# A decoder layer on one Trainium2 core: the pooling projection taken from x before its norm, with the token factors applied to the results

## The chip, the core and the metric

The kernel runs on one core of one Trainium2 chip. A core has five engines that work side by side, each through its own queue in order: TensorE (PE; matmuls, with its weight loads, PEld, overlapped), VectorE (DVE), ScalarE (ACT), GpSimd (POOL) and SyncE (SP), which here issues most transfers from HBM. Data lies in SBUF, 128 partitions wide; matmuls write PSUM, in banks of 128 x 512 floats. The metric is the time of one execution in microseconds (us) on the device, as the median of several.

## What is computed

One layer of a hybrid decoder, in fp32, on x of 512 tokens by 1024 channels. The input is normed, one wide projection gives everything that the three mixing branches and their gates need, and a gated FFN follows:

```python
def rmsnorm(x, g):
    xf = x.astype(jnp.float32)
    y = xf * lax.rsqrt(jnp.mean(xf * xf, axis=-1, keepdims=True) + NORM_EPS)
    return (y * g.astype(jnp.float32)).astype(x.dtype)

u = rmsnorm(x, ln1_g[i])
proj = u @ w_in[i]
q, k, v, pool_in, z, xbc, dt_raw, gate_pre = jnp.split(proj, split_idx, axis=-1)
y_a = dilated_attention_mixer(q, k, v, rel_bias) @ w_a[i]
y_b = pool_mixer(pool_in, pool_w[i], pool_scale[i]) @ w_b[i]
y_c = ssd_mixer(z, xbc, dt_raw, ...) @ w_c[i]
x = x + (gates[:, :, 0] * y_a + gates[:, :, 1] * y_b + gates[:, :, 2] * y_c) @ w_o[i]
x = x + conv_ffn(rmsnorm(x, ln2_g[i]), ...)
return rmsnorm(x, final_g)
```

`pool_mixer` takes means over the last 2, 4, 8 or 16 tokens of `pool_in` (1024 channels, four groups with a window each), subtracts `pool_in`, and multiplies by a small matrix per group. The change touches how u, and from it `pool_in`, come about. The factor of the norm belongs to a token, so it can be applied to a row of x before the projection, or to the token's results behind it.

## The kernel before

*Precision.* Every large product is made of three matmuls in a rounded format: each operand is split into a high part (rounded) and a low part (what the rounding left), and high x high, high x low and low x high are summed (`mm3`, L228). For a weight, ScalarE makes the high part (`cast`, L186, its line L195) and VectorE the low part (`lows`/`low`, L208 to L223, line L215). For the normed input, `uh` and `ul` (eight blocks of 128 channels, 512 tokens) are kept for the whole projection.

*Jobs.* The work is a list of jobs (`program`, L1422). A job has 1 MB of weights, say 256 columns: two chunks of 128 output channels by 512 tokens, 24 matmuls each. While a job runs, the low part of the next job's weights, the high part of the one after and the load of the third are put into the queues (`prepare`, L1624). There are two buffers of raw weights, three of high and two of low parts. The first four jobs are the pooling projection (eight chunks, `C_POOL`), then come the values of the first attention group (`v_jobs`, two jobs of 400 columns with tokens as output rows, each with half of the channel blocks), then queries and keys.

*Order.* The order on PE, ACT, DVE and POOL is that in which the program emits it (`manual_schedule`, L106); only SP is ordered by the framework. Work that trails behind a chunk is written as generators: `step()` (L156), called after each chunk, first runs what `second` holds (the second half of a cast), then starts one item of `waiting`, then moves each running generator to its next `yield`.

*Pooling chunk.* `pool_evac(m, ps)` (L771) copies the chunk out of its PSUM bank to `pu` on ScalarE (L775), GpSimd makes the window sums by doubling (L779 to L782: one to four additions `psw`), and two steps later VectorE subtracts (`pd`, L788), ScalarE rounds (`pdh`, L790) and VectorE makes the low part (`pdl`, L791). Four PSUM banks hold the chunks, so chunk m + 4 needs chunk m copied out.

*The start* (L1474 to L1613) is written out by hand. x arrives as four blocks of 128 tokens in two halves (`xin`). For blocks 0 and 1 ScalarE and VectorE sum the squares, a short chain (L1558 to L1564) gives a diagonal with the token factors, and TensorE turns and scales the block in one product with it (`turn_scale`, L1551). `turned` (L1519) multiplies by the gain, gives `uh` on ScalarE and `ul` on VectorE. Then `begin(n, lo, hi)` (L1526) runs chunks 0 to 3 of the pooling projection in halves of 256 tokens. Blocks 2 and 3 are scaled in place (L1587, L1589) and turned inside the second `begin`. GpSimd makes the low part of the first weights.

Of the kernel before, what the change touches and what calls it, by code (L numbers as in the profile page):

```python
# [16 lines left out]
P = 128  # L17
# [66 lines left out]
def trunk(ctx: ExitStack, tc, out, x, rel_bias, ln1_g, w_in, b_gate, w_a, pool_w, pool_scale, w_b,  # L84
# [682 lines left out]

    ramp = cpool.tile([P, 4, 16], F32, name="ramp")
    DP, YB = {}, {}

    def pool_evac(m, ps):  # L771
        g = m // 2
        w = 2 << g
        u = T("pu")
        act.copy(u, ps)  # L775
        cur, sh = u, 1
        while sh < w:
            nxt = T("psw")
            pool.tensor_tensor(nxt[:, sh:], cur[:, sh:], cur[:, :S - sh], OP.add)  # L779
            pool.tensor_copy(nxt[:, :sh], cur[:, :sh])  # L780
            cur, sh = nxt, sh * 2
        pool.tensor_tensor(cur[:, :w], cur[:, :w], ramp[:, g, :w], OP.mult)  # L782

        def later():
            yield
            yield
            d = T("pd")
            dve.scalar_tensor_tensor(d, cur, 1.0 / w, u, OP.mult, OP.subtract)  # L788
            dh, dl = T("pdh", F32R), T("pdl", F32R)
            act.copy(dh, d)  # L790
            dve.tensor_sub(dl, d, dh.bitcast(F32))  # L791
            DP[m] = (dh, dl)

        running.append(later())
# [678 lines left out]

    xin, warm = {}, small("warm", [P, 1])  # L1474

    def load_x(tb, eng=sp):
        for h in range(2):
# [12 lines left out]

    def warm_up(n):
        for i in range(n):
            pe.matmul(first[3][:, :P], ones, ones, start=True, stop=True)
# [11 lines left out]
    sp.dma_start(tri, c_tri)  # L1505
    rows_of_bias = bias_rows()

    def row_squares(tb, ss, n=1, eng=dve):

        for i in range(n):  # L1510
            squares(act, xin[tb + i, 0], ss[:, i:i + 1])
            squares(eng, xin[tb + i, 1], ss[:, n + i:n + i + 1])
        dve.tensor_tensor(ss[:, :n], ss[:, :n], ss[:, n:2 * n], OP.add)
        return ss[:, :n]

    def x_block(tb, k):
        return xin[tb, k // 4][:, (k % 4) * P:(k % 4 + 1) * P]

    def turned(k, lo, ps):  # L1519

        hh = uh[:, k, lo:lo + 256]
        act.mul(hh, ps, g1[:, k:k + 1])
        dve.scalar_tensor_tensor(ul[:, k, lo:lo + 256], ps, g1[:, k:k + 1], hh.bitcast(F32),
                                 OP.mult, OP.subtract)

    def begin(n, lo, hi, between=lambda early: None):  # L1526
        wh, wl = weights[n].split
        order = [(wh, uh, 0)]
        for k in range(1, KD):
            order += [(wh, uh, k), (wh, ul, k - 1)]  # L1530
        order.append((wh, ul, KD - 1))
        for part in (order, [(wl, uh, k) for k in range(KD)]):
            for a, b, k in part:
                for j in range(2):
                    pe.matmul(first[2 * n + j][:, lo:hi], a[:, k, j * P:(j + 1) * P], b[:, k, lo:hi],  # L1535
                              start=a is wh and b is uh and k == 0, stop=a is wl and k == KD - 1)
            between(part is order)
        if hi == S:
            for j in range(2):
                pool_evac(2 * n + j, first[2 * n + j])  # L1540
                step()


    warm_up(WARM)
    diag = [T("diag") for _ in range(2)]
    banks = [SM("uT") for _ in range(4)]

    def bank(k):
        return banks[k % 4][:, (k // 4) * 256:(k // 4) * 256 + 256]

    def turn_scale(tb, k):  # L1551
        pe.matmul(bank(k)[:, tb * P:(tb + 1) * P], x_block(tb, k), diag[tb][:, :P], start=True, stop=True)  # L1552

    for tb in range(2):
        s0, s1, v, sq, r, rt = (small(n, [P, 1]) for n in ("s0", "s1", "v", "sq", "r", "rt"))
        squares(act, xin[tb, 0], s0)
        squares((dve, act)[tb], xin[tb, 1], s1)
        dve.tensor_scalar(v, s0, 1.0 / D, EPS, OP.mult, OP.add)  # L1558
        dve.scalar_tensor_tensor(v, s1, 1.0 / D, v, OP.mult, OP.add)
        act.activation(sq, v, AF.Sqrt)  # L1560
        dve.reciprocal(r, sq)
        dve.scalar_tensor_tensor(rt, r, v, r, OP.mult, OP.mult)
        dve.tensor_scalar(rt, rt, -0.5, 1.5, OP.mult, OP.add)
        dve.tensor_scalar(diag[tb][:, :P], eye, r, rt, OP.mult, OP.mult)  # L1564
        if tb == 0:
            for k in range(KD):
                turn_scale(0, k)
    pe.transpose(first[2][:, :KD], g8[:KD, :P], eye[:KD, :KD])
# [8 lines left out]
    parts = lows(weights[1], 2)  # L1577


    ss = row_squares(2, small("ss", [P, 4]), 2)  # L1580
    next(parts)
    r = rstd_of(ss, 2, D)
    for tb in (2, 3):
        for h in range(2):
            t = xin[tb, h]
            if h:
                dve.tensor_scalar(t, t, r[:, tb - 2:tb - 1], None, OP.mult)  # L1587
            else:
                act.mul(t, t, r[:, tb - 2:tb - 1])  # L1589
    next(parts)  # L1590
    begin(0, 0, 256)

    def turns(early):
        if not early:
            return
        for k in range(4):
            banks[k] = SM("uT")
        for k in range(KD):
            for tb in range(2):
                pe.transpose(bank(k)[:, tb * P:(tb + 1) * P], x_block(2 + tb, k), eye)  # L1600
        for k in range(KD):
            turned(k, 256, bank(k))

    begin(1, 0, 256, turns)
    turn()
    fetch(weights[2])
    fetch(weights[3])
    begin(0, 256, S)
# [44 lines left out]
WARM = 12  # L1653

# [1 line left out]
_INS = ['x', 'rel_bias', 'ln1_g', 'w_in', 'b_gate', 'w_a', 'pool_w', 'pool_scale', 'w_b',  # L1656
# [26 lines left out]
```

## Time and profile before

| | us |
|---|---|
| median of 3 runs | 1042.7 (1042.38 to 1042.83) |
| the profiled execution, whole | 1044.23 |
| its span | 1042.4 |
| PE busy | 1030.2 |
| DVE busy | 645.8 |
| ACT busy | 466.9 |
| POOL busy | 151.1 |

The page gives the busy time of each engine, the chain of work that ended last, and groups of instructions by line. In a row of a group the columns are line, engine, operation, output and inputs by the program's names, shapes and count, then busy time in us and the mean of one in ns, then idle time of the engine just before and what ended it. In a row of the timeline the first number is the start in us, the second the length. A busy PE is not PE at its peak; GpSimd's spans are rough. The profile's times are those of one execution, whose whole time is a little over the span.

### The profile page before, as it was taken

What the parts mean: (1) busy time and instruction counts of PE and PEld (TensorE: products, weight loads), DVE (VectorE), ACT (ScalarE), POOL (GpSimd) and SP (SyncE); (2) the same over time, 40 slices, a digit from 0 to 9 for tenths busy, and PEclk for the clock granted to TensorE, in tenths of its full rate; (3) what the DMA queues carried; (4) which work ended last, traced back from release to release, by engine and by line L of the source; (5) the groups of instructions that cost most, each with busy time, mean ns of one, the idle gap of its engine ahead of it and who ended that gap; (6) DMA issues with size and microseconds to landing.
All of it is one profiled execution on the core that took longest, in us unless ns stands there. A gap on an engine that the chain in (4) does not pass through costs nothing.

```text
span 1042.4 us, 13096 instructions
## 1 busy us (share of the span) xinstructions
PE 1030.2 (99%) x5214; PEld 864.4 (83%) x5214; DVE 645.8 (62%) x864; ACT 466.9 (45%) x756; POOL 151.1 (14%) x125
## 2 busy tenths in 40 slices
PE   8999999999999999999999999999999999999997
PEld 8988878898888878888888888898888888878885
DVE  5563566684356658766768666767766566556645
ACT  5432554452464364557545233544444344433331
POOL 1680000000000004210152500002111111110110
PEclk9999999999999999999999999999999999999999
DMA  8345222126222344552243326642232322362332
GB/s 294 107 116 148 97 66 75 31 62 201 81 81 81 98 135 112 142 137 80 68 132 122 121 81 242 220 162 86 87 116 81 121 81 97 105 242 70 112 101 81
DMA packets 119788, 121.81 MB, mean 117 GB/s; under 512 B 5523, under 2 KB 101590, under 8 KB 119727
## 3 DMA queue, kind: packets, MB, share of 16 engines
q1 hardware_dynamic: 119135, 120.12, 36.4%
q8 instruction: 41, 0.67, 0.3%
q10 hardware_dynamic: 592, 0.86, 0.2%
q14 instruction: 20, 0.16, 0.1%
HBM read 115.07 MB, written 4.32 MB: 115 GB/s over the span
## 4 chain that ended last, share of the span: by engine, by line
PE 97%; DVE 1%; ACT 1%; DMA 0%; issue 0%; DVEq 0%; SPq 0%; ACTq 0%
PE pa L234 35%; PE pu L234 22%; PE pb L234 17%; PE pqk L234 9%; PE pa L1535 2%; PE p L234 2%; PE ps L662 1%; PE pu L1356 1%; PE ppw L234 1%; PE pt L690 1%; PE po L703 1%; PE py L988 1%; PE uT L1552 1%; PE pyo L995 1%; PE pst L974 0%; DMA xin<-in_x_dram 0%
## 5 line engine op out<-in xcount | busy, mean ns | idle before, releaser
L215 DVE TENSOR_TENSOR wl<-raw,wh 128x2048 fp32r<-128x2048 f32 (+3 forms) x95 | 217.1, 2287 | 73.9 <-ACT wh L195 41.7
L195 ACT CAST wh<-raw 128x1024 fp32r<-128x1024 f32 (+3 forms) x188 | 189.5, 1026 | 63.0 <-DVE raw L337 21.1
L234 PE MATMUL pa<-uh,wh 128*128 128x512 f32 x384 | 98.5, 398 | 0.0
L1192 DVE SCALAR_TENSOR_TENSOR hc<-pu,fcol,hc 128x510 f32<-128x510 f32 x88 | 65.8, 748 | 51.1 <-ACT hc L1189 49.5
L234 PE MATMUL pa<-ul,wh 128*128 128x512 f32 x384 | 94.9, 389 | 0.0
L234 PE MATMUL pa<-uh,wl 128*128 128x512 f32 x384 | 94.9, 389 | 0.0
L234 PEld LDWEIGHTS pa<-ul,wh 128*128 128x128 f32 x384 | 72.1, 188 | 15.2
L234 PEld LDWEIGHTS pa<-uh,wl 128*128 128x128 f32 x384 | 72.1, 188 | 15.0
L234 PE MATMUL pu<-uh,wh 128*128 128x512 f32 (+1 forms) x352 | 83.7, 380 | 0.0
L234 PE MATMUL pu<-ul,wh 128*128 128x512 f32 (+1 forms) x352 | 83.5, 379 | 0.0
L234 PE MATMUL pu<-uh,wl 128*128 128x512 f32 (+1 forms) x352 | 83.5, 379 | 0.0
L234 PEld LDWEIGHTS pa<-uh,wh 128*128 128x128 f32 x384 | 70.3, 188 | 14.7 <-issue 1.0
L234 PEld LDWEIGHTS pu<-uh,wh 128*128 128x128 f32 x352 | 64.1, 188 | 12.6 <-ACT uh L452 0.2
L234 PEld LDWEIGHTS pu<-ul,wh 128*128 128x128 f32 x352 | 64.2, 188 | 12.5
L234 PEld LDWEIGHTS pu<-uh,wl 128*128 128x128 f32 x352 | 64.2, 188 | 12.5
L1189 ACT ACTIVATE hc<-pu,fcol,fcol 128x512 f32<-128x512 f32 x40 | 31.2, 780 | 75.6 <-PE pu L234 75.4
L1197 POOL TENSOR_TENSOR hc<-hc 128x512 f32<-128x512 f32 x22 | 31.5, 1431 | 223.5 <-DVE hc L1192 169.3
L950 POOL TENSOR_TENSOR xd<-xc,dec 128x512 f32<-128x512 f32 x6 | 6.4, 1061 | 333.7 <-DVE xc L944 314.8
L1077 ACT ACTIVATE sg<-pa,col 128x512 f32<-128x512 f32 x24 | 16.5, 688 | 55.5 <-PE pa L234 48.7
L683 ACT ACTIVATE sb<-sb,both 128x128 f32<-128x128 f32 (+1 forms) x72 | 30.1, 419 | 23.5 <-DVE both L680 13.4
L234 PE MATMUL pqk<-uh,wh 128*128 128x512 f32 x144 | 36.9, 394 | 0.0
L234 PE MATMUL pqk<-ul,wh 128*128 128x512 f32 x144 | 36.3, 389 | 0.0
(355 smaller groups left out, 1765.1 us busy)
## 6 DMA issues: line engine op xcount, KB each, us to landing
raw<-in_w_in_dram SPq DMA_DIRECT2D x25, 1024.0 KB
raw<-in_ffn_w_up_dram SPq DMA_DIRECT2D x22, 1024.0 KB
raw<-in_w_in_dram SPq DMA_DIRECT2D x20, 512.0 KB
raw<-in_ffn_w_down_dram SPq DMA_DIRECT2D x10, 1024.0 KB
raw<-in_w_o_dram SPq DMA_DIRECT2D x8, 1024.0 KB
raw<-in_w_b_dram SPq DMA_DIRECT2D x4, 1024.0 KB
al<-ad SPq DMA_DIRECT2D x16, 256.0 KB
raw<-in_w_c_dram SPq DMA_DIRECT2D x4, 1024.0 KB
```

The source lines that it names most:

```text
L195: act.copy(job.high[:, :, o], job.raw[:, :, o])
L215: (eng or dve).tensor_tensor(l[:, :, o], job.raw[:, :, o], h[:, :, o].bitcast(F32), OP.subtract)
L234: pe.matmul(ps, l, r, start=first and n == 0, stop=last and n == total - 1)
L662: pe.matmul(pss[i][:, o:o + w * P], q[r, n * P:(n + 1) * P], k[r, kb * P:(kb + w) * P], start=True, stop=True)
L683: act.activation(sb[:, off:off + w * P], sb[:, off:off + w * P], AF.Exp, bias=nm[:, n, h:h + 1], accum_out=ls[:, n, h:h + 1])
L690: pe.transpose(pt[:, o:o + P], sb[:, o:o + P], eye)
L703: pe.matmul(po[DH * hh:DH * hh + DH, n * P:(n + 1) * P], V[g, kb + i][:, (2 * cc + hh) * DH:(2 * cc + hh + 1) * DH], probs[2 * cc + hh, mb ...
L1077: act.activation(s, ps, AF.Sigmoid, bias=col[:, o:o + 1])
L1189: act.activation(t, ps, AF.Identity, bias=ff["c1"][:, ff["b"] + m:ff["b"] + m + 1], scale=fw(2, m))
L1192: dve.scalar_tensor_tensor(t[:, sh:], ps[:, :S - sh], fw(k, m), t[:, sh:], OP.mult, OP.add)
L1197: pool.tensor_tensor(a, a, t, OP.mult)
L1535: pe.matmul(first[2 * n + j][:, lo:hi], a[:, k, j * P:(j + 1) * P], b[:, k, lo:hi], start=a is wh and b is uh and k == 0, stop=a is wl and ...
```

## The change

Raw x is turned by plain transposes as soon as it and the identity have landed; `turned` makes `RH` and `RL` (eight pairs of tiles) from it, raw x times gain. The pooling projection of all eight chunks reads `RH` and `RL`. The sums of squares run beside; their root chain and a matrix `dg` of four diagonals come after the second weights' low part, and a product of ones by `dg` spreads the 512 token factors over all partitions (`rb`). `pool_evac` now multiplies the PSUM bank by `rb` on VectorE instead of copying it on ScalarE. For the later projections `normed` makes `uh` and `ul` from `(RH + RL) * rb`, two channel blocks at a step, in four generators put into `waiting`. The high part of the first weights is made by VectorE in two halves between the first low parts; loads are issued in another order and spread over SP and ACT; the warm-up has 8 products, not 12.

```diff
 def pool_evac(m, ps):
-        act.copy(u, ps)
+        dve.tensor_tensor(u, ps, rb[0], OP.mult)
...
-        yield from jobs_a(w_in, C_POOL, 8, uhk, ulk, KD, pool_evac)
+        yield from jobs_a(w_in, C_POOL, 8, RH.get, RL.get, KD, pool_evac)
...
-    load_x(0)
-    load_x(1, act)
     act.dma_start(eye, c_eye)
+    load_x(0, (sp, act))
     act.dma_start(g8[:KD, :P], ln1_g[0].rearrange("(k p) -> k p", p=P))
+    load_x(1, (sp, act))
...
     fetch(weights[0], 2)
-    fetch(weights[1])
     load_x(2)
     load_x(3)
+    fetch(weights[1])
...
     def turned(k, lo, ps):
-        hh = uh[:, k, lo:lo + 256]
+        hh = RH[k][:, lo:lo + 256]
         act.mul(hh, ps, g1[:, k:k + 1])
-        dve.scalar_tensor_tensor(ul[:, k, lo:lo + 256], ps, g1[:, k:k + 1], hh.bitcast(F32),
+        dve.scalar_tensor_tensor(RL[k][:, lo:lo + 256], ps, g1[:, k:k + 1], hh.bitcast(F32),
                                  OP.mult, OP.subtract)
...
+    sq(0, 0, act)
+    turns = banks_of_two()
+    for k in range(KD):
+        transposed(0, k, turns[k])
     pe.transpose(first[2][:, :KD], g8[:KD, :P], eye[:KD, :KD])
     dve.tensor_copy(g1, first[2][:, :KD])
-    cast(weights[0], 2)
-    low(weights[0], 2, pool)
     for k in range(KD):
-        turn_scale(1, k % 2 * 4 + k // 2)
+        transposed(1, k, turns[k])
+    w0 = weights[0]
+    w0.high = whp.tile([P, KD, 256], F32R, name="wh", tag="wh")
     for k in range(KD):
-        turned(k, 0, bank(k))
+        if k in (1, 3):
+            o = slice((k - 1) * 64, (k - 1) * 64 + P)
+            dve.tensor_copy(w0.high[:, :, o], w0.raw[:, :, o])
+        turned(k, 0, turns[k])
+    low(w0, 2, pool)
+    highs(0, 0, 256)
+    for tb, h in ((0, 1), (1, 0), (1, 1)):
+        sq(tb, h, act)
...
+    dve.tensor_tensor(ss[:, 0, :], ss[:, 0, :], ss[:, 1, :], OP.add)
+    r = rstd_of(ss[:, 0, :], 4, D)
+    dg = T("dg")
+    dve.tensor_tensor(dg.rearrange("p (b t) -> p b t", b=4), eye.unsqueeze(1).to_broadcast([P, 4, P]),
+                      r.unsqueeze(2).to_broadcast([P, 4, P]), OP.mult)
+    highs(1, 0, 256)
+    for j in range(2):
+        lows_of(1, 0, 256, j)
+    ps = SM("prb")
+    pe.matmul(ps, ones, dg, start=True, stop=True)
+    rb.append(T("rb"))
+    act.copy(rb[0], ps)
     cast(weights[2])
+    for j in range(2):
+        pool_evac(j, first[j])
+    turn()
     low(weights[2])
-    begin(1, 256, S)
+    highs(1, 256, S)
+    for j in range(2):
+        lows_of(1, 256, S, j)
+
+    def normed(ks):
+        ts = []
+        for k in ks:
+            t = T("un")
+            dve.tensor_tensor(t, RH[k].bitcast(F32), RL[k].bitcast(F32), OP.add)
+            dve.tensor_tensor(t, t, rb[0], OP.mult)
+            act.copy(uh[:, k, :], t)
+            ts.append(t)
+        yield
+        for k, t in zip(ks, ts):
+            dve.tensor_sub(ul[:, k, :], t, uh[:, k, :].bitcast(F32))
+
+    fill([normed((k, k + 1)) for k in range(0, KD, 2)])
+    for j in range(2, 4):
+        pool_evac(j, first[j])
+        step()
     cast(weights[3])
     fetch(weights[4])
```

`highs` and `lows_of` are the former `begin` in two parts (high weights, low weights). In the changed kernel the lines of the new operations are L776 (`pu`), L1522 (transposes), L1518 (low part of raw x), L1536 and L1541 (matmuls of chunks 0 to 3), L1557 (first weights rounded), L1590 (`prb`), L1592 (`rb`), L1606 to L1612 (`un`, `uh`, `ul`).

More of the change, by code (lines that the diff above doesn't have):

```diff
@@ L1489, in trunk @@
     first = [MM("pa") for _ in range(4)]
-    def warm_up(n):
-        for i in range(n):
-            pe.matmul(first[3][:, :P], ones, ones, start=True, stop=True)
+    for i in range(WARM):
+        pe.matmul(first[3][:, :P], ones, ones, start=True, stop=True)
     fetch(weights[0], 2)
-    fetch(weights[1])
     load_x(2)
     load_x(3)
+    fetch(weights[1])
     sp.dma_start(ramp, c_ramp.partition_broadcast(P))
@@ L1506, in trunk, with sq @@
     rows_of_bias = bias_rows()
[L1508 to L1517, printed above, removed]
+    ss = cpool.tile([P, 2, 4], F32, name="ss")
+    def sq(tb, h, eng):
+        squares(eng, xin[tb, h], ss[:, h, tb:tb + 1])
@@ L1519, in turned @@
+    for k in range(KD):
+        RH[k], RL[k] = T("rh", F32R), T("rl", F32R)
     def turned(k, lo, ps):
-        hh = uh[:, k, lo:lo + 256]
+        hh = RH[k][:, lo:lo + 256]
         act.mul(hh, ps, g1[:, k:k + 1])
-        dve.scalar_tensor_tensor(ul[:, k, lo:lo + 256], ps, g1[:, k:k + 1], hh.bitcast(F32),
+        dve.scalar_tensor_tensor(RL[k][:, lo:lo + 256], ps, g1[:, k:k + 1], hh.bitcast(F32),
                                  OP.mult, OP.subtract)
-    def begin(n, lo, hi, between=lambda early: None):
-        wh, wl = weights[n].split
-        order = [(wh, uh, 0)]
-        for k in range(1, KD):
[L1530 to L1538, printed above, removed]
-            for j in range(2):
-                pool_evac(2 * n + j, first[2 * n + j])
-                step()
@@ L1544, in trunk, with transposed @@
[L1544 to L1567, printed above, removed]
+    def transposed(tb, k, ps):
+        pe.transpose(ps[:, tb % 2 * P:(tb % 2 + 1) * P], xin[tb, k // 4][:, (k % 4) * P:(k % 4 + 1) * P], eye)
@@ new lines, in banks_of_two, with highs @@
+    def banks_of_two():
+        banks = [SM("uT") for _ in range(4)]
+        return [banks[k % 4][:, (k // 4) * 256:(k // 4) * 256 + 256] for k in range(KD)]
+    def highs(n, lo, hi):
+        (wh, wl), pss = weights[n].split, first[2 * n:2 * n + 2]
+        order = [(RH, 0)]
+        for k in range(1, KD):
+            order += [(RH, k), (RL, k - 1)]
+        order.append((RL, KD - 1))
+        for m, k in order:
+            for j in range(2):
+                pe.matmul(pss[j][:, lo:hi], wh[:, k, j * P:(j + 1) * P], m[k][:, lo:hi],
+                          start=m is RH and k == 0, stop=False)
@@ L1568, in trunk, with lows_of @@
+    def lows_of(n, lo, hi, j):
+        for k in range(KD):
+            pe.matmul(first[2 * n + j][:, lo:hi], weights[n].split[1][:, k, j * P:(j + 1) * P],
+                      RH[k][:, lo:hi], start=False, stop=k == KD - 1)
+    sq(0, 0, act)
+    turns = banks_of_two()
+    for k in range(KD):
+        transposed(0, k, turns[k])
     pe.transpose(first[2][:, :KD], g8[:KD, :P], eye[:KD, :KD])
     dve.tensor_copy(g1, first[2][:, :KD])
[L1570 to L1571 removed]
     for k in range(KD):
[L1573 removed]
+        transposed(1, k, turns[k])
@@ L1576, in trunk @@
+    lows_of(0, 0, 256, 1)
+    for k in range(KD):
+        turned(k, 256, turns[k])
     cast(weights[1], 2)
[L1577 to L1582, printed above, removed]
+    highs(0, 256, S)
     for tb in (2, 3):
         for h in range(2):
[L1585 to L1605, printed above, removed]
+            sq(tb, h, (act, dve)[h])
+    low(weights[1])
+    for j in range(2):
+        lows_of(0, 256, S, j)
```

14 lines of the change are left out of this document (10 added, 4 removed).

## The prediction

> **What bounds the kernel now.** I read the page first, then the chain of waits over the first 70 us, then the busy time by stretch.
>
> ```profile
> span 1042.4 us, 13096 instructions
> PE 1030.2 (99%) x5214; PEld 864.4 (83%) x5214; DVE 645.8 (62%) x864; ACT 466.9 (45%) x756; POOL 151.1 (14%) x125
> PE 97%; DVE 1%; ACT 1%; DMA 0%; issue 0%; DVEq 0%; SPq 0%; ACTq 0%
> ```
>
> TensorE is busy for 99% of the span and makes 97% of the chain that ended last, so a step counts only if it makes TensorE begin earlier, do more, or wait. The chain of waits for the stage that the change touches (start, length, what):
>
> ```profile
> 7.97 3.65 PE uT L1552 x16
> 11.62 0.15 PE pa L1568
> 11.78 1.98 PE uT L1552 x16
> 13.76 9.60 PE pa L1535 x80
> 23.36 1.75 PE uT L1600 x16
> ...
> 38.96 21.79 PE pa L234 x96
> 60.75 4.39 PE pb L234 x24
> ```
>
> From 13.5 us on TensorE never stops: four pooling chunks (L1535) until 38.8, four more (L234) until 60.6, then the attention values (pb). There are 13.5 us in front of it to shorten, and 47 us behind it that other engines must keep covered. The busy time in these stretches (columns: length; PE, PEld, DVE, ACT, POOL busy; granted clock; DMA share; GB/s):
>
> ```profile
> 13.50:38.80 25.30, 25.16 (x213) 24.98 (x211) 14.39 (x33) 12.78 (x26) 5.55 (x7) 1.00 0.54 184
> 38.80:60.60 21.80, 21.80 (x99) 18.04 (x98) 14.06 (x13) 9.83 (x14) 20.48 (x26) 1.00 0.44 125
> ...
> 0.00:7.00 7.00, 4.60 (x24) 4.41 (x24) 1.24 (x8) 2.56 (x6) 0.43 (x5) 1.00 0.76 230
> 7.00:8.00 1.00, 0.05 (x1) 0.05 (x1) 0.83 (x5) 1.00 (x4) 0.00 (x0) 0.98 1.16 349
> 8.00:11.00 3.00, 3.00 (x14) 3.00 (x15) 1.04 (x5) 2.16 (x4) 1.48 (x1) 0.50 1.10 379
> 11.00:12.00 1.00, 1.00 (x7) 0.86 (x7) 0.17 (x1) 0.00 (x0) 1.00 (x2) 0.81 1.08 405
> 12.00:13.00 1.00, 1.00 (x11) 1.00 (x11) 0.04 (x1) 0.54 (x2) 1.00 (x1) 1.00 1.06 410
> ```
>
> VectorE works 14.06 of the 21.80 us in the second stretch: 7.7 us are free. This row decides.
>
> **The change, part by part.**
>
> *Start of TensorE.* Removed ahead of the transposes are the squares, the two root chains and the diagonals of token blocks 0 and 1; x is turned raw, by plain transposes. What they wait for is now x itself. As built, the SP queue carries x(0, left), half of the first weights, x(1, left), the other half; the ACT queue identity, x(0, right), gains, x(1, right), as many issues as before. So x(1, left) stands behind 0.064 + 4 x 0.262 + 0.524 = 1.64 MB; the row 0 to 7 us gives 230 x 7.0 = 1.61 MB at 7.0, hence 7.1, and with 0.4 for the signal (an allowance) block 1 is turned at 7.5. The rows from there on:
>
> ```profile
> 9.52 4.68 POOL L215 TENSOR_TENSOR wl<-raw,wh 128x1024 fp32r<-128x1024 f32 x2 [8.56 <-ACT wh L195]
> 11.71 2.05 PE L1552 MATMUL uT<-diag,xin 128*128 128x128 f32 x16
> 12.46 3.27 ACT L1522 ACTIVATE uh<-uT,g 128x256 fp32r<-128x256 f32 x8 [2.07 <-PE uT L1552]
> 12.96 3.39 DVE L1523 SCALAR_TENSOR_TENSOR ul<-uT,g,uh 128x256 fp32r<-128x256 f32 x8 [0.98 <-ACT uh L1522]
> 13.52 0.72 PE L1535 MATMUL pa<-uh,wh 128*128 128x256 f32 x4
> ...
> L1523 DVE SCALAR_TENSOR_TENSOR ul<-uT,g,uh x16: 473/476/485, 13.0 to 27.7; 128x256 fp32r<-128x256 f32 x16
> ...
> L1587 DVE TENSOR_SCALAR xin<-xin,r 128x512 f32<-128x512 f32 x2 | 0.9, 482 | 0.0
> L215 DVE TENSOR_TENSOR wl<-raw,wh 128x1024 fp32r<-128x1024 f32 x2 | 2.4, 1217 | 0.0
> ```
>
> First turn to first scaled copy is 0.75 (11.71 to 12.46), to the first low part 0.5 more: 8.75, and one low part (0.48) ends at 9.2. New on VectorE is the rounding of the first weights in two halves of 128x1024 (L1557), one behind low part 0, one behind low part 2. No row shows that copy; 2 x 0.48 from L1587 and 1.22 from the 128x1024 subtraction bound it, I take 1.0 (nearest in form). Half 0 ends at 10.2 and the first matmul goes; the second needs half 1, whose turn comes at 10.2 + 2 x 0.48 = 11.2. But GpSimd by then subtracts half 0 (4.68 / 2 = 2.34, from 10.2 to 12.6). Whether the two exclude each other, these rows tell (minimum, median, maximum of one form; then two pairs in order of time):
>
> ```profile
> L332 DVE TENSOR_TENSOR sbl<-sb,sbh x8: 681/1232/1784, 191.6 to 792.9; 128x512 fp32r<-128x512 f32 x8
> ...
> 36.08 2.29 DVE L215 TENSOR_TENSOR wl<-raw,wh 128x2048 fp32r<-128x2048 f32 x1 [7.70 <-ACT wh L195]
> 36.16 2.26 POOL L780 COPY psw<-pu 128x1 f32<-128x1 f32 x1
> 38.29 0.68 DVE L788 SCALAR_TENSOR_TENSOR pd<-psw,pu 128x512 f32<-128x512 f32 x1
> ...
> 48.98 1.04 POOL L779 TENSOR_TENSOR psw<-pu 128x511 f32<-128x511 f32 x1
> 49.06 1.50 DVE L788 SCALAR_TENSOR_TENSOR pd<-psw,pu 128x512 f32<-128x512 f32 x1 [0.36 <-POOL psw L782]
> ```
>
> The same VectorE subtraction takes 0.68 or 1.78 us; a GpSimd copy of one column lasts as long as VectorE's low part beside it; and `pd` grows from 0.68 to 1.50 beside a GpSimd addition. An operation with all its operands in SBUF waits for GpSimd's to end, and the other way round. The low parts L1523, which read PSUM, keep 473 to 485 ns, though three ran beside GpSimd at 13 to 14 us. The copy has its operands in SBUF: I let it wait, to 12.6 + 1.0 = 13.6. The second matmul then stands against 13.52 + 0.12 before: nothing gained. Free of the wait it comes at 12.2: -1.4.
>
> The granted clock is 0.50 from 8 to 11 us, after 2.3 us of a quiet TensorE. In the changed kernel it has only some twenty transposes between the warm-up and 13.6, so it likely starts at half rate. One half-rate spell lasted 3.4 us (7.97 to 11.4: 0.81 over the slice from 11 to 12 us), which costs 1.7 at most and nothing at least; I take 1.0. The Trainium skill (TensorE: Matmul & The Clock Gate, Part 4: PE-mode transpose) says that transposes do not engage the full clock; the rows cannot tell, since before the first ones were ordinary matmuls by a diagonal. By that rule this term would be 1.7, not 1.0, and the sum 0.7 higher.
>
> *Added to TensorE*: one ones-by-diagonal product (`prb`, L1590). Its kind exists at L1058:
>
> ```profile
> 541.81 1.02 PE L1058 MATMUL prb<-dg,ones 128*128 128x512 f32 x2
> ```
>
> I take 0.9 without the drain. Chunks, second-half transposes and the columns' transpose stay: 0. Moved past others at no cost: the loads of x(2), x(3) ahead of the second weights (all 4.2 MB are in by about 14 us at 230 to 410 GB/s; the second weights are first rounded some 9 us after the first matmul), the three squares of ScalarE behind the scaled copies (2.4 us, before the second half's copies at 6 us after the start), and the root chain with `dg`, done some 3 us before its product. Start in all: 0 + 1.0 + 0.9 = +1.9; ends -1.4 + 0.9 = -0.5 and +2.6.
>
> *VectorE behind the first four chunks.* Added: eight multiplies from PSUM (`pu`, L776, instead of ScalarE copies), and eight groups of one addition, one multiply (L1606, L1607) and one subtraction (L1612): 32 operations of 128x512. Prices:
>
> ```profile
> L404 DVE TENSOR_TENSOR uf<-uh,ul 128x512 f32<-128x512 f32 x8 | 5.1, 683 | 0.0
> L453 DVE TENSOR_TENSOR ul<-uT,uh 128x512 fp32r<-128x512 f32 x8 | 5.0, 681 | 3.8 <-ACT uh L452 3.8
> L1090 DVE TENSOR_TENSOR sg<-sg,pa 128x512 f32<-128x512 f32 x16 | 11.0, 685 | 16.0 <-PE pa L234 13.2 <-DMA raw<-in_w_o_dram 2.6
> ...
> L788 DVE SCALAR_TENSOR_TENSOR pd<-psw,pu 128x512 f32<-128x512 f32 x8 | 8.8, 1096 | 7.2 <-POOL psw L782 7.2
> L215 DVE TENSOR_TENSOR wl<-raw,wh 128x1600 fp32r<-128x1600 f32 x2 | 4.5, 2234 | 0.0
> ...
> 42.42 0.76 DVE L791 TENSOR_TENSOR pdl<-pd,pdh 128x512 fp32r<-128x512 f32 x1 [0.69 <-ACT pdh L790]
> ...
> L790 ACT CAST pdh<-pd 128x512 fp32r<-128x512 f32 x8 | 5.0, 622 | 13.0 <-DVE pd L788 13.0
> L195 ACT CAST wh<-raw 128x2048 fp32r<-128x2048 f32 x2 | 3.8, 1912 | 0.0
> ...
> L779 POOL TENSOR_TENSOR psw<-pu 128x511 f32<-128x511 f32 x8 | 8.3, 1038 | 20.1 <-ACT pu L775 20.1
> ```
>
> So 32 x 0.685 = 21.9 us go into a queue with 7.7 us free per 21.8. What counts is the last thing that TensorE asks for. As built, VectorE runs `pu` 2, four of `un` (normed 0, 1), `pu` 3, two of `ul`, four of `un`, the low part of the fourth weights, `pu` 4, `pd`/`pdl` 0 to 2, two `ul`, four `un`, `pu` 5, `pd`/`pdl` 3, two `ul`, four `un`, and only then the low part of the first attention weights (128x1600). Free of GpSimd: 4 `pu` 2.7; 16 `un` 10.9; 6 `ul` 4.1; 4 `pd` and 4 `pdl` 5.5; the ScalarE trip between them 4 x 0.69 = 2.8; low parts 2.3 and 1.8; and the wait for the fourth weights' rounding, which ScalarE does behind its copy of the fourth normed row, 0.62 + 1.91 = 2.5. That is 32.6; neighbours overlap by 0.08 (36.08 + 2.29 against 38.29), 28 times: 30.4. It begins 1.0 before chunk 3 ends (call that end E) and so ends at E + 29.4. TensorE wants this low part after four chunks (60.6 - 38.8 = 21.8) and two thirds of a first group (1.5): E + 23.3. TensorE waits 6.1 us.
>
> GpSimd's sums of chunks 2 to 5 fall into that time: ten additions of 1.04. Each can hold VectorE for 0 to 0.9. Before, eight `pd` averaged 1.10 instead of 0.68, 3.4 us over twenty such additions, 0.2 each, but VectorE was then idle a third of the time. I take 0.5 each: +5.0, ends +0 and +9.0. TensorE's wait: 11.1, ends 6.1 and 15.1. Nothing gives it back later, TensorE being the chain to the end. Hidden are ScalarE's eight additional copies (it loses eight of `pu` for them), the later fetches, and, just, chunk 7's bank (`pu` 7 about 4.8 us behind that low part, wanted 5.1 behind it).
>
> *The clock again.* A wait of 6 us or more is longer than the 2.3 us after which the clock halved; after it TensorE restarts at half rate for about 3.4 us: +1.7, ends 0 and 3.4. The Trainium skill agrees (same page, Part 1: The HAM clock gate): a window of about 3.4 us, halved after an idle one; without it the sum would be 1.7 lower.
>
> *Sum*: 1.9 + 11.1 + 1.7 = +14.7. The profiled execution took 1044.23 (span 1042.4 and 1.8 around it), so 1058.9; it stands 1.5 above the median of 1042.7, to which I add the same 14.7: 1057.4.
>
> **Rivals.**
> A, no contention: VectorE's new operations slip in between GpSimd's. For it: low parts of 2.29 beside GpSimd; against it: 1.50 instead of 0.68. 1.9 + 6.1 + 1.7: 1052.4.
> B, full contention: every addition of GpSimd gets between two VectorE operations. For it: 1.78 in L332's spread; against it: the mean price before, 0.2. 1.9 + 15.1 + 1.7 = 18.7, and chunk 7's bank comes about 1.5 late: 1062.9. The Trainium skill (SBUF — State Buffer, the section on two separate sides) has this rule: the pair of ports is locked for a whole instruction, and the other engine blocks.
> C, not slower: the VectorE queue keeps up, and only the start speaks: -0.5 to +1.9, say 1043.5. Its place is the low part of the attention weights; it must end 6.1 us sooner, so 34 operations of 128x512 would have to average 0.50, not 0.68. L404 and L453, the same operations at 0.68, speak against it. With the start at its best end it is 1042.2.
> D, the start does not move at all, because x(1, left) still lands behind weights: that is in the forecast.
>
> **How the numbers follow.** Forecast (contention in part) 0.55, own range 1054 to 1061; A 0.19; B 0.19; C 0.05 (0.04 of it within 0.2%, that is 2.1 us, about what can be told from no change); 0.02 for something faster. Eight in ten: from A with no half clock behind the wait (1050) less its best start (-2.4) to B, and half of its upper clock end: 1048 to 1064. Slower 0.94, same 0.04, faster 0.02.
>
> **What would show it.** Start right: second L1536 matmul at 12 to 14 us, clock 0.50 around it. VectorE right: idle time of PE before the attention values (`pb`) put down to VectorE's low part, 6 us or more, `un` near 0.68 to 1.5, VectorE above 90% between 40 and 70 us. Wrong would be a TensorE without a gap there, or a gap at another place: at chunk 6 (the fourth weights' rounding, which I have 1 to 2 us late, absorbed by the longer wait behind), or through chunk 7's bank.

## The result and the profile after

The changed kernel takes 1061.03 us (median of six, 1060.15 to 1061.84) beside 1042.99 us (median of six, 1042.38 to 1044.02) for the kernel before in the same comparison: a ratio of 1.0172, with a 95% interval from 1.0158 to 1.0185. It is slower by 18 us. The profiled execution took 1061.32, its span 17.1 us more than that of before. The profiled execution of before, 1044.23, lies 1.2 us above this median of before, that of the changed kernel 0.3 above its own; 17.1 + 1.2 - 0.3 = 18.0, so the spans and the medians tell the same story. The executions of before whose clock is on record lie in two groups, 1042.3 to 1043.0 at a mean granted clock of 0.998 to 0.999 and 1043.8 to 1045.8 at 0.996 to 0.997, and the profiled one, at 0.997, is of the second.

The same lines of the page as those that opened the prediction, now of the changed kernel:

```profile
span 1059.5 us, 13075 instructions
PE 1034.6 (98%) x5192; PEld 865.9 (82%) x5192; DVE 666.3 (63%) x882; ACT 465.1 (44%) x753; POOL 154.5 (15%) x125
PE 91%; DVE 4%; ACT 2%; DMA 1%; issue 1%; ACTq 0%; DVEq 0%
```

TensorE's share of the chain fell from 97% to 91%; VectorE's rose from 1% to 4%, ScalarE's from 1% to 2%. VectorE's busy time rose by only 20.5 us of 1040; its share of the whole span, 63%, says nothing of the loss. The chain of waits over the first 110 us says where it is (start, length, what):

```profile
11.26 2.20 DVE wh L1557
13.50 6.65 PE pa L1536 x31
...
35.31 0.86 PE prb L1590 x2
...
52.31 1.90 ACT wh L195
54.24 2.29 DVE wl L215
...
75.12 1.83 DVE wl L215
...
76.99 5.01 PE pb L234 x16
```

Before, this chain was TensorE's alone from 13.76 us on, but for 0.13 us. Now the stretch from 41.1 to 77.0 us belongs to VectorE and ScalarE, and its last piece is the low part of the first attention weights (`wl`, L215). TensorE's own rows, from the timeline (in brackets the idle time just before, and what ended it), first the changed kernel, then the rows of before that they are compared with:

```profile
41.87 2.00 PE L234 MATMUL pa<-rh,wh 128*128 128x512 f32 x8
54.26 2.11 PE L234 MATMUL pa<-rh,wh 128*128 128x512 f32 x8 [1.33 <-ACT wh L195]
68.59 1.70 PE L234 MATMUL pb<-wh,uh 128*128 128x400 f32 x4 [3.16 <-ACT wh L195]
76.99 1.70 PE L234 MATMUL pb<-wl,uh 128*128 128x400 f32 x4 [5.36 <-DVE wl L215]
96.83 1.98 PE L234 MATMUL pqk<-uh,wh 128*128 128x512 f32 x8
```

```profile
38.80 2.00 PE L234 MATMUL pa<-uh,wh 128*128 128x512 f32 x8
62.05 0.90 PE L234 MATMUL pb<-wl,uh 128*128 128x400 f32 x4
79.97 0.39 PE L234 MATMUL pqk<-uh,wh 128*128 128x512 f32 x1
```

The queries and keys (`pqk`) begin 16.9 us later than before, and from there on both kernels run alike, since the spans differ by 17.1. In front of them are three waits: 1.33 for the fourth weights' rounding, 3.16 for the second half of the attention weights' rounding on ScalarE (L195), 5.36 for VectorE's low part. Chunk 4, the point E of the prediction, begins at 41.87 in the same view (38.80 before; the chain of waits puts it some 0.16 later, so what is counted from E goes by the timeline). So of the 16.9 us, 3.1 are lost before E and 13.8 behind it.

The granted clock by stretches of 2 us (columns: length; PE, PEld, DVE, ACT, POOL busy; clock; DMA share; GB/s):

```profile
8.00:10.00 2.00, 0.66 (x4) 0.42 (x4) 0.61 (x2) 1.12 (x4) 0.00 (x0) 0.84 1.10 343
...
18.00:20.00 2.00, 2.00 (x13) 2.00 (x13) 0.00 (x0) 0.00 (x0) 0.00 (x0) 0.60 0.80 215
20.00:22.00 2.00, 2.00 (x20) 2.00 (x19) 0.00 (x0) 0.00 (x0) 0.00 (x0) 1.00 1.06 392
...
66.00:68.00 2.00, 0.00 (x0) 0.00 (x0) 1.97 (x4) 1.29 (x3) 0.13 (x1) 0.85 0.00 0
...
80.00:82.00 2.00, 2.00 (x10) 1.73 (x9) 2.00 (x3) 0.00 (x0) 1.92 (x3) 0.74 1.10 286
82.00:84.00 2.00, 2.00 (x10) 0.99 (x11) 1.33 (x2) 0.58 (x2) 1.92 (x3) 1.00 0.02 4
40.00:70.00 30.00, 25.51 (x117) 21.02 (x117) 24.35 (x31) 9.43 (x13) 20.21 (x24) 0.96 0.20 55
```

All slices between 10 and 18 us, and between 68 and 80 us, are at 0.50. Taking each mixed slice as part half rate, part full rate (0.84 over two us is 0.64 us at half rate), the spells run from 9.36 to 19.60 and from 67.4 to 81.04. The last row is the stretch that decides: VectorE is busy for 24.35 of 30 us.

### The profile page after: what moved, and what is told of

Its sections match the earlier page's. It is cut to its first block, busy times and chain, and to the rows that moved or that the text cites. A ratio compares the mean times of both kernels' runs of the same rounds, so it can differ in the third digit from the quotient of the medians.

```text
span 1059.5 us, 13075 instructions
## 1 busy us (share of the span) xinstructions
PE 1034.6 (98%) x5192; PEld 865.9 (82%) x5192; DVE 666.3 (63%) x882; ACT 465.1 (44%) x753; POOL 154.5 (15%) x125
## 4 chain that ended last, share of the span: by engine, by line
PE 91%; DVE 4%; ACT 2%; DMA 1%; issue 1%; ACTq 0%; DVEq 0%
PE pa L234 32%; PE pu L234 22%; PE pb L234 17%; PE pqk L234 9%; PE p L234 2%; PE pa L1536 2%; PE ps L662 1%; PE ppw L234 1%; PE pt L690 1%; PE po L703 1%; PE py L989 1%; DVE un L1607 1%; ACT wh L195 1%; PE pa L1541 1%; DVE wl L215 1%; DMA raw<-in_ffn_w_up_dram 1%
## 5 line engine op out<-in xcount | busy, mean ns | idle before, releaser
L215 DVE TENSOR_TENSOR wl<-raw,wh 128x2048 fp32r<-128x2048 f32 (+2 forms) x94 | 216.0, 2300 | 67.3 <-PE pb L234 30.5
L195 ACT CAST wh<-raw 128x1024 fp32r<-128x1024 f32 (+3 forms) x186 | 187.4, 1026 | 67.7 <-DVE raw L337 21.1
L234 PE MATMUL pa<-uh,wh 128*128 128x512 f32 x352 | 90.6, 399 | 0.0
L234 PE MATMUL pa<-ul,wh 128*128 128x512 f32 x352 | 87.0, 389 | 0.0
L234 PE MATMUL pa<-uh,wl 128*128 128x512 f32 x352 | 86.9, 389 | 0.0
L234 PEld LDWEIGHTS pa<-ul,wh 128*128 128x128 f32 x352 | 66.1, 188 | 14.0
L234 PEld LDWEIGHTS pa<-uh,wl 128*128 128x128 f32 x352 | 66.1, 188 | 13.7
L234 PEld LDWEIGHTS pa<-uh,wh 128*128 128x128 f32 x352 | 64.3, 188 | 13.5 <-issue 1.0
L683 ACT ACTIVATE sb<-sb,both 128x128 f32<-128x128 f32 (+1 forms) x72 | 30.1, 418 | 23.5 <-DVE both L680 13.4
```

The source lines that it names most:

```text
L195: act.copy(job.high[:, :, o], job.raw[:, :, o])
L215: (eng or dve).tensor_tensor(l[:, :, o], job.raw[:, :, o], h[:, :, o].bitcast(F32), OP.subtract)
L234: pe.matmul(ps, l, r, start=first and n == 0, stop=last and n == total - 1)
L683: act.activation(sb[:, off:off + w * P], sb[:, off:off + w * P], AF.Exp, bias=nm[:, n, h:h + 1], accum_out=ls[:, n, h:h + 1])
```

## The experiments

The theory: the loss behind E is the length of VectorE's queue up to that low part, GpSimd's window sums stretching it; the start gains nothing because VectorE's second rounding waits for GpSimd; and half rates of the clock at the start and behind the wait come on top. The rivals: contention is nothing, or everything; the loss comes from somewhere else in the new order; the clock spells are an accompaniment without a price. Every edit is against the changed kernel unless it is said otherwise.

**Without the normalising of the later projections' input.**

```diff
-            t = T("un")
-            dve.tensor_tensor(t, RH[k].bitcast(F32), RL[k].bitcast(F32), OP.add)
-            dve.tensor_tensor(t, t, rb[0], OP.mult)
+            t = RH[k].bitcast(F32)
             act.copy(uh[:, k, :], t)
```

> Leaves out the normalising of the rows for the later projections: the sixteen additions and multiplies `un` are gone, uh is a rounded copy of RH, ul the rest, so VectorE keeps only the eight subtractions of the eight groups. Theory (VectorE's queue): 10.9 us of operations and the wait of ScalarE's fourth cast behind them go from the ledger, the low part of the first attention weights ends at about E + 19 instead of E + 35, ahead of the E + 23.3 at which TensorE wants it; no gap of TensorE between 40 and 80 us, and only the start is left: +3 us against the kernel before, 1045 to 1047. Rival (the extra multiply out of PSUM and the banks it holds up make the wait): TensorE still waits 4 us or more ahead of the attention values, 1052 or more. Rival (GpSimd's window sums, which start late, are what VectorE waits for): the same gap stays, 1058 or more.

Measured: 1047.64 us (1046.63 to 1048.0), ratio to before 1.0043 (1.0028 to 1.0058). The chain of waits:

```profile
42.12 21.79 PE pa L234 x96
63.91 4.39 PE pb L234 x24
```

Sixteen VectorE operations gone, and every wait behind E is gone with them: chunks 4 to 7 and the values follow one another as they did before. 13.4 of the 18 us go; the time is 0.6 above the range that was forecast. The low part ends 22.0 us behind E in the timeline, where 19 had been forecast, still ahead of the E + 23.3 at which TensorE asks for it. What is left is mainly the late start. A cause elsewhere in the new order (transfers, the ScalarE copies, which are still there) falls.

**Without GpSimd's window sums.**

```diff
-        while sh < w:
-            nxt = T("psw")
-            pool.tensor_tensor(nxt[:, sh:], cur[:, sh:], cur[:, :S - sh], OP.add)
...
-        pool.tensor_tensor(cur[:, :w], cur[:, :w], ramp[:, g, :w], OP.mult)
```

> Leaves out the window sums on GpSimd (pd is made of pu alone); every operation of VectorE stays. Theory (VectorE's queue, lengthened by GpSimd in part): without contention the low part ends at E + 29.4, so TensorE waits about 6 us instead of 10.3, and the time falls by 4 to 5 us, to 1056 or 1057. Rival A (contention costs nothing): within 1 us of the changed kernel, 1060 to 1062. Rival B (GpSimd is the cause of most of the wait): the gap falls under 2 us, 1050 or less.

Measured: 1056.80 us (1056.22 to 1057.15), ratio 1.0131 (1.0114 to 1.0148). The chain of waits around the low part:

```profile
70.64 1.83 DVE wl L215
...
72.51 5.42 PE pb L234 x16
```

Here chunk 4 begins at 41.96, so the low part ends 30.5 us behind E. In the changed kernel it ends at 76.95, which is 35.1 behind E. The difference, 4.6 us, is what GpSimd's sums cost VectorE. It is neither nothing nor the 9.0 of full contention. The single operations show how it comes about (timeline of the changed kernel, two neighbours on VectorE and an addition of GpSimd between them):

```profile
47.59 0.68 DVE L1606 TENSOR_TENSOR un<-rh,rl 128x512 f32<-128x512 f32 x1
47.68 1.48 POOL L780 TENSOR_TENSOR psw<-pu 128x511 f32<-128x511 f32 x1
48.30 1.41 DVE L1607 TENSOR_TENSOR un<-un,rb 128x512 f32<-128x512 f32 x1
```

A multiply (L1607) lasts 0.69, or 1.41 when an addition of GpSimd is in its way: a step, not a general slowing. Up to the low part four of the eight multiplies last 1.41; with the smaller additions to `ul`, `un` and `pdl` the rows sum to the same 4.6.

**Keeping TensorE busy at the start**: twelve more products of ones between the transposes and the first matmuls.

```diff
+    warm_up(1)
     for k in range(KD):
         transposed(1, k, turns[k])
+        if k == 3:
+            warm_up(1)
+    warm_up(10)
```

> Adds twelve products of ones to TensorE while it has nothing to do (one behind the gains' transpose, one in the middle of block 1's transposes, ten behind them), so that no quiet window lies ahead of the first matmuls; all else as in the changed kernel. Theory (half clock from 13.5 to 19.6 us costs 2.9 us at the start): the first 31 matmuls take 3.7 instead of 6.6 us, chunk 4 begins 2 to 3 us earlier and the whole is 2 to 3 us shorter, 1058 to 1059. Rival (the low parts of raw x, 0.48 us each on VectorE, pace those matmuls anyway): under 0.5 us. Rival (VectorE's backlog does not begin with chunk 3 but with the loads, so an earlier start is waited away): chunk 4 earlier but the same total, 1061.

Measured: 1059.35 us (1058.04 to 1060.36), ratio 1.0156 (1.0141 to 1.0172). The chain of waits:

```profile
13.30 3.98 PE pa L1539 x31
38.26 0.69 DVE pu L776
```

The 31 matmuls that took 6.65 us take 3.98: 2.7 us is the price of half rate at the start, and it has one. VectorE's `pu` of chunk 2, with which its long queue begins, moves from 41.10 to 38.26, 2.8 us; but the time falls by only 1.7, a little less than forecast. Most of the rest is given back behind the wait: in this run the half rate there ended at 79.96 (the changed kernel's spell at 81.04), 5.8 us after TensorE resumed at 74.15, where it was 4.05 us in the changed kernel; the 1.8 us more at half rate cost 0.9.

**GpSimd's subtraction of the first weights in one piece**, so that it comes behind both roundings.

```diff
-    low(w0, 2, pool)
+    low(w0, 1, pool)
```

> GpSimd subtracts the first weights in one piece, which cannot begin before both halves are rounded; all else as in the changed kernel. Theory (VectorE's second rounding took 2.27 instead of 0.68 us because GpSimd held the common port): it takes 0.68 us again and the second matmul comes at 11.9 instead of 13.5, 1.6 earlier; the whole gains 0.8 to 1.6, less what a longer half-rate spell takes. Rival (the second rounding was late because of its load): it stays at 2.2 us or begins later, and nothing changes.

Measured: 1059.37 us (1058.28 to 1061.2), ratio 1.0159 (1.0144 to 1.0174). The chain of waits:

```profile
11.26 0.61 DVE wh L1557
11.91 5.70 PE pa L1536 x31
```

The second rounding takes 0.61 instead of 2.20 us, at the same place with the same operands; the matmuls resume at 11.91 instead of 13.50. The wait for GpSimd is shown. Chunk 4 comes 2.5 earlier by the timeline (39.35), because half rate also ends earlier at the start; the time falls by only 1.7, because behind the wait TensorE, resuming at 74.49, is at half rate for 6.2 us instead of 4.05.

**Both edits of the start**, with seven products behind the transposes.

> Both changes to the start at once: nine products of ones keep TensorE busy ahead of the first matmuls, and GpSimd subtracts the first weights in one piece. Theory (two separate losses, 2.9 us of half clock and 1.6 us of the held port): chunk 4 begins near 37.4 us instead of 41.9, 1.4 ahead of the kernel before, and the total falls by 3 to 4.5, to 1056.5 to 1058; the wait ahead of the attention values stays as long as it was, about 9 to 10 us. Rival (one of the two only hides behind the other): no better than the better of the two alone, 1059.3.

Measured: 1058.59 us (1058.14 to 1059.24), ratio 1.0146 (1.0131 to 1.0162). The forecast of 1056.5 to 1058 failed by 0.6: chunk 4 begins at 38.51 by the timeline, not at 37.4. The two gains do not add up, and the chain of waits names what is late next:

```profile
11.87 4.60 POOL wl L215
16.51 1.22 PE pa L1544 x8
```

The matmuls with the low weights (L1544) now wait for GpSimd's single piece, 0.7 us.

**The pooling's `pd` and `pdl` later**, eight steps behind their chunk instead of two, so that they leave the queue ahead of the attention weights' low part.

```diff
         def later():
-            yield
-            yield
+            for _ in range(8):
+                yield
             d = T("pd")
```

> The subtraction of each pooling chunk on VectorE (pd, pdl) comes eight steps behind its chunk instead of two, so behind the low part of the first attention weights; nothing is left out, all else as in the changed kernel. Theory (it is the order of VectorE's queue, not its capacity, that makes TensorE wait): eight operations and four trips to ScalarE, 7.6 us, leave the ledger, the low part ends near E + 26, TensorE waits 2 to 3 us there instead of 5.4 behind 3.2, and the time falls to 1047 to 1051. Rival (VectorE is simply over its capacity until the queries and keys): the deferred work makes TensorE wait later by as much, 1058 or more.

Measured: 1056.19 us (1055.37 to 1057.31), ratio 1.0122 (1.0108 to 1.0136). This expectation failed: 1047 to 1051 had been forecast. The chain of waits:

```profile
66.55 1.41 DVE un L1607
...
69.92 1.82 DVE wl L215
...
71.79 5.70 PE pb L234 x16
```

The low part ends 29.9 us behind E (71.74 - 41.87), where 26 had been forecast. Eight operations and their ScalarE trips, 8.3 us of the ledger, left the queue, but the multiplies (L1607) behind chunk 4, free of GpSimd in the changed kernel at 65 to 67 us, now stretch to 1.41. The new theory: the contention grew. Its test is the next kernel.

**The same without the window sums.**

> As e6, with the window sums on GpSimd left out (pd is made of pu alone). In e6 the low part of the first attention weights ended at E + 29.9 instead of the E + 26 that I had worked out. Theory (with no trips to ScalarE in VectorE's queue GpSimd's sums collide with every second operation, so contention is 8 us there and not 4): without them it ends at E + 22, before E + 23.3, TensorE has no wait ahead of the attention values, and the total is that of the start alone, 4 to 5 us above the kernel before. Rival (the ledger is wrong by 4 us in another place, such as the fourth weights' rounding): a wait of 4 us or more is left.

Measured: 1048.03 us (1046.64 to 1049.04), ratio 1.0043 (1.0027 to 1.0060). The chain of waits:

```profile
41.80 21.79 PE pa L234 x96
63.58 4.39 PE pb L234 x24
```

E and the low part in the timeline:

```profile
41.63 2.00 PE L234 MATMUL pa<-rh,wh 128*128 128x512 f32 x8
62.31 1.82 DVE L215 TENSOR_TENSOR wl<-raw,wh 128x1600 fp32r<-128x1600 f32 x1
```

Without GpSimd the low part ends 22.5 us behind E (62.31 + 1.82 - 41.63), just ahead of the E + 23.3 at which TensorE asks for it, and there is no wait. So GpSimd costs VectorE 29.9 - 22.5 = 7.4 us in this order, 4.6 in the changed kernel's. The single rows give the same: with late `pd` seven of the eight multiplies (L1607) last 1.41, four in the changed kernel. There the three additions that begin at 57.21, 59.30 and 61.35 overlap VectorE's waits for ScalarE, 0.69 each, and the `pdl` behind them last 0.75 to 0.76, some 0.07 more than alone; with late `pd` additions at the same times stand beside `ul` and `un`. That pauses let GpSimd pass almost free is what these rows suggest; no run tested it by itself.

**A better order, nothing left out**: both edits of the start, `pd` and `pdl` late, and, new,

```diff
-    fill([normed((k, k + 1)) for k in range(0, KD, 2)])
+    cast(weights[3])
+    items = [normed((k, k + 1)) for k in range(0, KD, 2)]
+    fill(items[:3])
+    waiting.extend([FREE, items[3]])
...
-    cast(weights[3])
```

so that the fourth weights' rounding goes ahead of the normed rows, and the last pair of normed rows is made a step later, behind the low part that TensorE asks for.

> A version made of what the runs point to, nothing left out: the start of e5, the subtraction of the chunks deferred as in e6, the fourth weights' high part ahead of the normed rows in ScalarE's queue, and the last pair of normed rows one step later, behind the low part of the first attention weights. Theory: the low part ends near E + 21, before E + 23.3, so TensorE has no gap from 12 us on, and the start is 1.4 us ahead of the kernel before: 1041 to 1042.5, 0.1% faster than before and 1.8% faster than the changed kernel. Rival (contention with GpSimd grows when VectorE's queue has no trips to ScalarE to fill): a wait of 2 us or more is left, 1044 or more.

Measured: 1044.22 us (1043.75 to 1045.09), ratio 1.0006 (0.9998 to 1.0015). The chain of waits:

```profile
12.04 4.62 POOL wl L215
16.70 1.22 PE pa L1544 x8
...
38.87 21.79 PE pa L234 x96
60.66 4.49 PE pb L234 x24
```

The total failed the forecast of 1041 to 1042.5: chunk 4 begins where it did before (38.87, against 38.96), not 1.4 ahead, after the same wait for GpSimd's single piece. But the 32 operations are all still there, and none of the waits behind E. What cost the time was their place in VectorE's queue ahead of the low part, not their number alone.

**The kernel before with a longer warm-up** (18 products instead of 12), to see how much of any gain is the clock's.

```diff
-WARM = 12
+WARM = 18
```

> The kernel before with 18 products of ones in the warm-up instead of 12, nothing else. Theory (the granted clock of 0.50 from 8 to 11.4 us lengthens the first scaled transposes by 1.8 us): TensorE is not quiet between 5.6 and 7.9 us, they run at the full clock, the first matmul comes 1 to 1.8 us earlier, 1041 to 1042. Rival (the start waits for ScalarE's rounding of the first weights, to 10.4 us, anyway): under 0.5 us, 1042.5 or more.

Measured: 1042.85 us (1042.49 to 1044.28), ratio 0.9993 (0.9984 to 1.0002). The chain of waits:

```profile
8.00 2.02 PE uT L1552 x16
...
37.34 21.79 PE pa L234 x96
```

The sixteen products that turn and scale x take 2.02 us instead of 3.65 at half rate, and chunk 4 is 1.6 earlier than in the profiled execution of before. The median moves by less than the interval can tell, and the forecast of 1041 to 1042 failed. Nine of the eleven executions (1042.5 to 1043.2) lie close to the first of the two groups of before, 1042.3 to 1043.0. That the first group has no half rate at the start would explain both; no profile shows one of its executions.

**The better order with both roundings side by side** on VectorE and GpSimd's subtraction in two halves again, five products of warm-up.

```diff
-        if k in (1, 3):
-            o = slice((k - 1) * 64, (k - 1) * 64 + P)
-            dve.tensor_copy(w0.high[:, :, o], w0.raw[:, :, o])
+        if k == 1:
+            for o in (slice(0, P), slice(P, 2 * P)):
+                dve.tensor_copy(w0.high[:, :, o], w0.raw[:, :, o])
```

> As e8, but the two roundings of the first weights stand next to each other on VectorE, behind the first low part, and GpSimd subtracts in two halves again; five products of ones instead of seven behind the transposes. In e5 and e8 the single subtraction of 4.6 us ended at 16.5 us, one us after TensorE wanted it. Theory: the second rounding follows the first before GpSimd can take the port, both are done near 11.1 us, GpSimd's first half near 13.5, ahead of its use at 15; chunk 4 begins near 36.8 us, 2 us ahead of the kernel before, and the whole is 1.5 to 2.2 us shorter than before (0.15 to 0.2%). Rival (GpSimd gets in between the two all the same): second matmul near 13 us, chunk 4 near 38.5, within 0.5 us of before.

Measured: 1042.45 us (1042.04 to 1044.08), ratio 0.9989 (0.9981 to 0.9998). The chain of waits:

```profile
9.85 1.21 DVE wh L1564 x2
...
11.11 3.98 PE pa L1539 x31
...
36.98 21.79 PE pa L234 x96
58.77 4.50 PE pb L234 x24
```

Both roundings together take 1.21 us, the matmuls begin at 11.11, and chunk 4 at 36.98. Of the kernels that leave nothing out it is the fastest: 1.8% below the changed kernel, and 0.11% below the kernel before, where 0.15 to 0.2% had been forecast. It doesn't stand out from the kernel before with the longer warm-up (0.9993), nor from the first group of the executions of before; whether taking raw x into the projection is worth anything beyond an unbroken clock isn't settled.

## Why the prediction was right, and where its sizes were off

The forecast was 1057.4, with 1048 to 1064 around it; measured 1061.0. That lies at the upper end of the forecast's own range (1054 to 1061) and nearer to rival B's 1062.9; it is the runs, not the number, that decide between the two. The forecast mechanism, a wait for VectorE's low part of the first attention weights, is the one that the trace and the runs show. Its terms, forecast and measured in the profiled execution:

| step of the sum | forecast | measured |
|---|---|---|
| second L1536 matmul against before | 0 (13.6) | 0 (13.50) |
| half rate at the start | +1.0 | +2.7 |
| `prb` | +0.9 | +0.9 |
| rest of the shift of E (not pursued) | none | -0.5 |
| low part late: ledger without GpSimd | +6.1 (E + 29.4) | +7.2 (E + 30.5) |
| low part late: contention | +5.0 | +4.6 |
| half rate behind the wait | +1.7 | +2.0 |
| sum | +14.7 | +16.9 |

How the measured column comes about: 2.7 is 6.65 - 3.98; 0.9 is the row at 35.31; the fourth is what is left of the 3.07 us by which E moved. The low part ended at E + 35.1 against E + 23.3, so it was 11.8 late, of which 4.6 come from the kernel without sums. From there to `pqk` it is 19.84 us (96.83 - 76.99), 2.0 more than from 62.1 to 79.97 before, and half of the 4.05 us at half rate.

The forecast fell short by 3.6 us. 2.2 of these lie in the table (16.9 - 14.7) and 0.2 behind `pqk`. The other 1.2 come from the last step of the sum: its terms were worked out against the rows of an execution that stands 1.2 to 1.5 above the median, and were then added to the median.

*The start.* That nothing is gained, because the second rounding waits for GpSimd's half, was right: 2.20 us beside GpSimd, 0.61 without. That the second matmul came at 13.50, against 13.6, is in part luck. The last transposes of block 1 began at 8.51, waiting for x, not at 7.5, and the first low part ended at 9.87 instead of 9.2; the price of each copy was taken too high (1.0, measured 0.6 in the chain), and the two errors nearly cancel. The mis-sized term is the clock: +1.0 was taken, between 0 and 1.7, because one spell before had lasted 3.4 us. Here the spell lasted 10.2 us, and 6.1 of it lay on matmuls. The rule of the Trainium skill (TensorE: Matmul & The Clock Gate, Part 4: PE-mode transpose) that transposes do not engage the full clock would have given 1.7 and came nearer; by itself it doesn't give 2.7, because that was thought of as one spell of 3.4 us.

*VectorE's ledger.* The order of the work was as written, and the end without GpSimd was 1.1 late. One row of the ledger was too kind: neighbours were let overlap by 0.08 each, 28 times. A multiply (L1607) reads the sum that the operation before it has just made, and a pair takes 0.61 + 0.02 + 0.69 = 1.32 us in the kernel without sums, not 2 x 0.685 - 2 x 0.08 = 1.21; over eight pairs that is 0.9. The other 0.2 is where it begins: `pu` of chunk 2 starts 0.8 before E, not 1.0. Contention at 5.0, between 0 and 9.0, measured 4.6. Rivals A (none) and B (all) fall with it, and rival C fell with the result.

*The places of the waits.* A wait of 1 to 2 us at chunk 6 was named, and is there with 1.33. The wait of 3.16 us for the second half of the attention weights' rounding on ScalarE wasn't; it adds nothing to the sum, since the low part further on would be waited for anyway. But it splits the wait: 5.36 us are put down to the low part, where 6 or more had been named as the sign. The statement that VectorE would be above 90% busy between 40 and 70 us was wrong: 24.35 of 30 is 81%. It was at odds with the ledger itself, which holds 5.3 us of waits for ScalarE. A queue can be the limit while its engine is idle a fifth of the time.

*What stays open.* The kernels without any wait behind E (without `un`, and with late `pd` and no sums) stand 4.8 and 5.0 above before, though in the chain of waits chunk 4 comes only 3.2 and 2.8 later than in the profiled execution of before (42.12 and 41.80 against 38.96). Most of the difference is how far the profiled executions lie from their medians: their spans are only 3.8 and 3.1 above that of before (1046.2 and 1045.5 against 1042.4). The remaining 0.6 and 0.3, which arise after the queries and keys have begun, aren't explained.

## What to carry to other kernels

When work moves into an in-order queue, add up that queue from the edit to the next thing that the limiting engine asks for, with its waits for other engines, and compare with the time at which it is asked for; the engine's share over the span (62% before, 63% after) tells nothing. The same 32 operations made TensorE lose 13.8 us behind E or nothing, depending on where in the queue they stand. Price a long pause of TensorE above its length: here the one at the start cost 2.7 us and the one ahead of the low part 2.0 in half rate, while the wait of 1.33 us at chunk 6 cost none (clock 1.00 from 51 to 58 us).

## What the runs showed of the hardware

*Half rate came in multiples of 3.4 us, and each spell ended with a stretch of that length that TensorE filled whole.* Ends and lengths of the spells, worked out from slices of 2 us as above: changed kernel 10.2 us (three times 3.41) and 13.65 (four times); GpSimd's subtraction late, 9.04 to 15.88, 6.8 (two times); without sums, 70.64 to 77.48, 6.8; before, one of 3.4. In the changed kernel the two spells begin 58.0 us apart (9.36 and 67.4), 17 times 3.41, as if the steps ran on without regard to the work. Counted back from the end of the first spell in steps of 3.41 (19.60, 16.19, 12.78), TensorE resumed at 13.50 inside a step, and only the next step, busy throughout, brought the full rate back. The fullest step here that didn't was busy for 2.8 of 3.41 us (73.90 to 77.31, GpSimd's subtraction late). By that, as an estimate, a resumed TensorE stays at half rate for 3.4 to 6.8 us and loses 1.7 to 3.4, depending on when it resumes; the runs show 3.97 us after resuming at 11.91, 4.05 at 76.99, 5.8 at 74.15, 6.1 at 13.50, 6.2 at 74.49. The Trainium skill (TensorE: Matmul & The Clock Gate, Part 1: The HAM clock gate) has the window of about 3.4 us that runs on its own; these runs agree with it, while its budget of the first 3.4 us is only the lower end here.

*Copies in SBUF wait for GpSimd whole.* A VectorE copy of 128x1024 lasts 0.68 us alone and 2.27 beside GpSimd's subtraction (timeline of the changed kernel), which agrees with the Trainium skill (SBUF — State Buffer, the section on two separate sides), by which VectorE and GpSimd share a pair of ports that is locked for a whole instruction:

```profile
9.79 0.68 DVE L1557 CAST wh<-raw 128x1024 fp32r<-128x1024 f32 x1
10.55 2.34 POOL L215 TENSOR_TENSOR wl<-raw,wh 128x1024 fp32r<-128x1024 f32 x1 [9.59 <-DVE wh L1557]
11.17 2.27 DVE L1557 CAST wh<-raw 128x1024 fp32r<-128x1024 f32 x1
```

What I had not expected is that taking other work off VectorE raised what GpSimd's sums cost it, from 4.6 to 7.4 us.
